# Gate and up projections in seven block products of half width, weight sums formed by adding DMA

## The chip, the cores and the metric

One NeuronCore of a Trainium2 chip runs the whole kernel. The metric is device microseconds of one execution: before the change the median of three runs is 753.54 us (752.19 to 753.91). TensorE is called PE, its weight loads PEld, VectorE DVE, ScalarE ACT, GpSimd POOL and SyncE SP.

## The reference

An encoder block on 512 tokens of width 1024, all in float32: a normed input is projected, goes through two attentions and a gated output projection, and a SwiGLU mixer follows with 2816 inner columns:

```python
h = rms_norm(x, norm_ffn[l])
x = x + (jax.nn.silu(h @ w_gate_ffn[l]) * (h @ w_up_ffn[l])) @ w_down_ffn[l]
```

The change concerns these two lines. The result is the final norm of `x`.

## The kernel before, in words

**Split products.** Every float32 operand is held as two float32r tiles: `hi`, a rounded copy that ACT casts (line 68), and `lo`, the rest, which DVE subtracts (line 75). A product takes three matmuls, hi·hi, hi·lo and lo·hi (`mm3`, lines 88 to 90). `load_unit` (line 77) loads 128x1024 floats of a weight on SP's queue into one of three `raw` buffers and splits it into one of five `whi`/`wlo` pairs of the pool `wp`.

**Before the mixer.** Projections and the attentions come first (group A, then four heads `attend_b`, lines 390 to 421). In a head of `attend_b`, POOL scales the exponentials (line 395), DVE combines two of them (line 399), PE transposes the result (line 361). `weave` (line 439) takes one step of each of several generators in turn, so that the columns of the gates (`gate_col`, line 426, 24 matmuls of 512 columns each) lie between the steps of the heads. The two last heads are woven at lines 465 and 466. Then the output projections follow (lines 488 to 512, 561 to 580); `norm_tile` (line 531) norms one block of 128 tokens, transposes it on PE and leaves its split in `hh` and `hl` (128x8x512: eight blocks of the model width, 512 tokens).

**Gate and up.** `ffn_in` (line 605) makes one of 22 column blocks f of gate and up: for each of the two, eight `mm3` with 512 tokens moving, 48 matmuls in all. For f = 0 and 1 it runs on 256 tokens at a time, so that it can start before the last norm. ACT makes the sigmoid, DVE two products, and the activation block is kept in `acts`.

```python
for f in range(2, NF):
    ffn_in(f, 0, S, *gu(f))
    if f % 2 == 1:
        sums_a(f // 2)
        down0(f // 2 - 1)
```

**Down, in seven products.** The down projection is already done as seven products of 2x2 blocks instead of eight. `sums_a` (line 626) keeps sums of activation blocks in SBUF for each pair of f. `down0` (line 667) loads both column halves of a weight unit, does two of the seven products at once (12 matmuls of 512 columns for each pair of f) and calls `sums_w` (line 647): four DVE differences of 128x512 per pair, each stored from POOL's queue to DRAM (`td`). After the loop `product` (line 704) does the other five products: `weights` loads the sums back, `stat` splits the sums of activations.

**Order.** The program gives each engine its instructions in an order fixed ahead of the run: a planner goes through them in program order as priority, with its own estimates of their times. On the chip every engine works in that order and waits at each instruction for what it needs.

## Time and profile before

| | before |
|---|---|
| median of the runs shown | 753.54 us |
| the profiled execution: its own time | 752.75 us |
| the profiled execution: span of its trace | 751.0 us |
| mean granted PE clock | 0.996 of full speed |
| busy share of the span: PE, PEld | 97%, 83% |
| busy share: DVE, ACT, POOL | 65%, 49%, 17% |
| HBM read, written | 81.20 MB, 13.63 MB |

The span runs from the first to the last instruction. Around it lie 1.75 us (752.75 less 751.0) that the profile does not show, and the profiled execution is 0.79 us below the median. Matmuls are pipelined: the duration of one (389 ns with 512 columns) is longer than the distance between the starts of two, and the distance is what counts for a long row of them.

### The profile page before, as it was taken

The page shows a single profiled execution, that of the slowest core. Times are in us where ns is not written, and L with a number is a line of the kernel's source. Part 1 is how long each engine was busy: PE and PEld are TensorE (multiplying, and loading weights), DVE is VectorE, ACT ScalarE, POOL GpSimd, SP SyncE. Part 2 cuts the span into 40 slices and gives each one's busy share as a digit, 9 for nine tenths or more (in the row PEclk, how much of TensorE's full clock was granted, in tenths as well). Part 3 has the DMA queues.
Part 4 walks back from the last instruction along what each step waited for, and adds up shares of the span by engine and source line. Part 5 has one row for each costly group of instructions (what it writes and reads, how often), then busy time and mean ns, then how long its engine had stood idle before and what let it go on. Part 6 is the DMA issues. An engine that isn't in the chain of part 4 may idle for free.

```text
span 751.0 us, 10105 instructions
## 1 busy us (share of the span) xinstructions
PE 730.7 (97%) x3687; PEld 625.1 (83%) x3687; DVE 491.5 (65%) x811; ACT 367.6 (49%) x664; POOL 128.9 (17%) x170
## 2 busy tenths in 40 slices
...
GB/s 324 79 72 70 57 44 84 1 43 49 65 140 58 57 59 82 168 113 124 143 29 113 224 179 154 145 196 195 168 130 179 196 180 147 215 140 197 190 222 57
DMA packets 29634, 95.50 MB, mean 127 GB/s; under 512 B 3856, under 2 KB 4112, under 8 KB 29584
## 3 DMA queue, kind: packets, MB, share of 16 engines
...
q14 instruction: 21, 0.17, 0.1%
HBM read 81.20 MB, written 13.63 MB: 126 GB/s over the span
## 4 chain that ended last, share of the span: by engine, by line
PE 94%; DVE 2%; DMA 2%; ACT 1%; issue 1%; POOLq 0%; POOL 0%; ACTq 0%; DVEq 0%
PE pu L90 5%; PE pg L90 5%; PE pg L89 5%; PE pu L89 5%; PE pg L88 5%; PE pu L88 5%; PE gt L89 4%; PE gt L88 4%; PE gt L90 4%; PE p L89 3%; PE p L88 3%; PE p L90 3%; PE acc_b L89 3%; PE acc_b L88 3%; PE acc_b L90 3%; PE pp L88 2%
## 5 line engine op out<-in xcount | busy, mean ns | idle before, releaser
L88 PE MATMUL pg<-hh,whi_fg 128*128 128x512 f32 (+1 forms) x192 | 71.4, 372 | 0.0
L90 PE MATMUL pu<-hh,wlo_fu 128*128 128x512 f32 (+1 forms) x192 | 71.4, 372 | 0.0
L89 PE MATMUL pg<-hl,whi_fg 128*128 128x512 f32 (+1 forms) x192 | 71.3, 371 | 0.0
L90 PE MATMUL pg<-hh,wlo_fg 128*128 128x512 f32 (+1 forms) x192 | 71.3, 371 | 0.0
L88 PE MATMUL pu<-hh,whi_fu 128*128 128x512 f32 (+1 forms) x192 | 71.3, 371 | 0.0
L89 PE MATMUL pu<-hl,whi_fu 128*128 128x512 f32 (+1 forms) x192 | 71.3, 371 | 0.0
L654 POOL DMA_DIRECT2D td<-tw x44 | 24.0, 546 | 269.8 <-DVE tw L653 220.4
L68 ACT CAST whi_fg<-raw_fg 128x1024 fp32r<-128x1024 f32 x22 | 23.2, 1054 | 76.9 <-issue 43.4
L68 ACT CAST whi_fu<-raw_fu 128x1024 fp32r<-128x1024 f32 x22 | 23.2, 1054 | 74.1 <-issue 70.1
L88 PE MATMUL gt<-xgh,whi_g 128*128 128x512 f32 x128 | 50.6, 395 | 0.0
L90 PE MATMUL gt<-xgh,wlo_g 128*128 128x512 f32 x128 | 50.5, 395 | 0.0
L89 PE MATMUL gt<-xgl,whi_g 128*128 128x512 f32 x128 | 50.4, 394 | 0.0
L89 PE MATMUL acc_b<-wlo_b,xgh 128*128 128x384 f32 x128 | 43.6, 341 | 0.0
L90 PE MATMUL acc_b<-whi_b,xgl 128*128 128x384 f32 x128 | 43.4, 339 | 0.0
L88 PE MATMUL acc_b<-whi_b,xgh 128*128 128x384 f32 x128 | 43.3, 339 | 0.0
L75 DVE TENSOR_TENSOR wlo_fg<-raw_fg,whi_fg 128x1024 fp32r<-128x1024 f32 x22 | 26.9, 1222 | 24.5 <-ACT whi_fg L68 24.3
L89 PEld LDWEIGHTS pu<-hl,whi_fu 128*128 128x128 f32 x192 | 36.2, 188 | 6.3
L89 PEld LDWEIGHTS pg<-hl,whi_fg 128*128 128x128 f32 x192 | 36.2, 188 | 6.3
L88 PEld LDWEIGHTS pg<-hh,whi_fg 128*128 128x128 f32 x192 | 36.2, 188 | 6.2
L88 PEld LDWEIGHTS pu<-hh,whi_fu 128*128 128x128 f32 x192 | 36.2, 188 | 6.2
L90 PEld LDWEIGHTS pg<-hh,wlo_fg 128*128 128x128 f32 x192 | 36.2, 188 | 6.2
L90 PEld LDWEIGHTS pu<-hh,wlo_fu 128*128 128x128 f32 x192 | 36.2, 188 | 6.2
...
## 6 DMA issues: line engine op xcount, KB each, us to landing
td<-tw POOLq DMA_DIRECT2D x44, 256.0 KB, 4.5
raw_fg<-in_w_gu_dram SPq DMA_DIRECT2D x22, 512.0 KB, 4.4
raw_fu<-in_w_gu_dram SPq DMA_DIRECT2D x22, 512.0 KB, 3.2
raw_t<-td SPq DMA_DIRECT2D x20, 512.0 KB, 3.9
raw_g<-in_w_in_dram SPq DMA_DIRECT2D x16, 512.0 KB, 3.2
...
raw_r<-in_w_down_dram SPq DMA_DIRECT2D x11, 512.0 KB, 4.1
raw_l<-in_w_down_dram SPq DMA_DIRECT2D x11, 512.0 KB, 3.3
```

Of the source, the lines that this page charges most:

```text
L68: a.copy(dst, src)
L75: v.tensor_tensor(out=dst, in0=src, in1=hi.bitcast(F32), op=ALU.subtract)
L88: pe.matmul(acc, lhsT=lh, rhs=rh, start=start, stop=False, skip_group_check=loose)
L89: pe.matmul(acc, lhsT=lh, rhs=rl, start=False, stop=False, skip_group_check=loose)
L90: pe.matmul(acc, lhsT=ll, rhs=rh, start=False, stop=stop, skip_group_check=loose)
L654: g.dma_start(tdram[i][p][:, k * S:(k + 1) * S], t)
```

## The change

The gate and up blocks of f = 2 to 21 are computed as seven products of 2x2 blocks: rows are gate and up, the inner index is halved, and the tokens are halved to 256 (`H`). A product is four `mm3`, 12 matmuls with 256 tokens moving; `g12`, `g5`, `g63`, `g7`, `g4` issue them for one f and the next in turn. Three PSUM banks take part: `q` (two buffers) collects four of the products one after the other and is read out between them. f = 0 and 1 are as before.

The sums of the moving side, `th`/`tl`, are made once after the last norm, at lowered priority (`LATER`). The sums of weights come for each f from two host-made arrays: `w_x0` is loaded on SP's queue, `w_x1` is added to it in SBUF by a DMA on POOL's queue; DVE adds two more, so that three units and a half unit are split per f instead of two.

The sums of the down weights leave DVE: 24 copies from DRAM to DRAM and 24 adding DMAs, all on POOL's queue, in 26 steps, 18 of them woven into the last two heads and 8 before the output projections. The sums of activations are written to DRAM on SP's queue (five stores of 128 KB per pair of f) and loaded again by `stat`. The last product now goes on in the banks `p1` instead of banks of its own. The cut diff:

```diff
...
+    def wblock(i, j, p):
+        n = min(2, NU - 2 * p)
+        return w_down[NU * j + 2 * p:NU * j + 2 * p + n, :, i * S:(i + 1) * S].rearrange("k p s -> p k s")
+
+    def tcopy(i, p, src):
+        return lambda: tc.keep_in_program_order(g.dma_start(tdram[i][p][:, :src.shape[1], :], src))
+
+    def tadd(i, p, src):
+        return lambda: tc.keep_in_program_order(g.dma_start(tdram[i][p][:, :src.shape[1], :], src, accum_op=ALU.add, max_dma_last_dim=4 * S))
+
+    def tsum(i, p):
+        n = min(2, NU - 2 * p)
+        first = (wblock(0, 0, p), wblock(1, 1, p), wblock(0, 1, p), wblock(1, 0, p))[i]
+        second = (wblock(0, 1, p), tdram[0][p][:, :n, :], wblock(1, 1, p), tdram[1][p][:, :n, :])[i]
+        return tcopy(i, p, first), tadd(i, p, second)
+
+    tsums = [tsum(i, p) for i in (0, 2, 1, 3) for p in range(NP)]
+    tsums = [(lambda k=k: [tsums_[k][0]() if k < len(tsums_) else None, tsums_[k - 2][1]() if k > 1 else None]) for tsums_ in [tsums] for k in range(len(tsums) + 2)]
...
-    weave(attend_b(2, *nxt), steps(todo[4:9]))
-    weave(attend_b(3, *nxt1), steps(todo[9:13]))
+    weave(attend_b(2, *nxt), steps(todo[4:9]), steps(tsums[:9]))
+    weave(attend_b(3, *nxt1), steps(todo[9:13]), steps(tsums[9:18]))
...
+        for f in tsums[18 + 2 * qd:20 + 2 * qd]:
+            f()
...
+            a.copy(hraw[2 * (tt // 2) + i][:, :, tt % 2 * P:(tt % 2 + 1) * P], p3)
...
+    with tc.high_priority(offset=-LATER):
+        traw = {"1": hraw[2], "2": hraw[3], "3": hraw[0], "4": hraw[1]}
+        v.tensor_tensor(out=hraw[2], in0=hraw[0], in1=hraw[2], op=ALU.subtract)
+        v.tensor_tensor(out=hraw[3], in0=hraw[3], in1=hraw[2], op=ALU.add)
+        v.tensor_tensor(out=hraw[0], in0=hraw[3], in1=hraw[0], op=ALU.subtract)
+        v.tensor_tensor(out=hraw[1], in0=hraw[3], in1=hraw[1], op=ALU.subtract)
+        for n in "1234":
+            h, l = th[n]
+            if n == "2":
+                split_scaled(h, l, traw[n], -1.0)
+            else:
+                split_hi(h, traw[n])
+                split_lo(l, traw[n], h)
...
+    def load_sums(f):
+        raw = wp.tile([P, UNIT], F32, tag="raw", bufs=3, name=f"raw_a{f}")
+        nc.sync.dma_start(raw, w_gu[2 * f])
+        early = f == 2
+        x = wp.tile([P, UNIT], F32, tag="raw", bufs=3, name=f"x{f}") if early else tp_.tile([P, UNIT], F32, tag="x", bufs=3, name=f"x{f}")
+        nc.sync.dma_start(x, w_x0[f])
+        g.dma_start(x, w_x1[f], accum_op=ALU.add)
+        r22 = tp_.tile([P, S], F32, tag="r22", bufs=3, name=f"r22_{f}")
+        nc.sync.dma_start(r22, w_gu[2 * f + 1][:, S:])
+        hi, lo = split_unit(raw, f"a{f}")
+        w = wts[f] = {"11": (hi[:, :S], lo[:, :S]), "12": (hi[:, S:], lo[:, S:])}
+        hi, lo = split_unit(x, f"x{f}")
+        w["s1"], w["s3"] = (hi[:, :S], lo[:, :S]), (hi[:, S:], lo[:, S:])
+        y = wp.tile([P, UNIT], F32, tag="raw", bufs=3, name=f"y{f}") if early else tp_.tile([P, UNIT], F32, tag="y", bufs=1, name=f"y{f}")
+        v.tensor_tensor(out=y[:, :S], in0=x[:, :S], in1=raw[:, :S], op=ALU.add)
+        v.tensor_tensor(out=y[:, S:], in0=y[:, :S], in1=raw[:, S:], op=ALU.add)
+        hi, lo = split_unit(y, f"y{f}")
+        w["s2"], w["s4"] = (hi[:, :S], lo[:, :S]), (hi[:, S:], lo[:, S:])
+        h = sp_.tile([P, S], F32R, tag="h22", bufs=3, name=f"h22_{f}")
+        l = sp_.tile([P, S], F32R, tag="l22", bufs=3, name=f"l22_{f}")
+        split_hi(h, r22)
+        split_lo(l, r22, h)
+        w["22"] = (h, l)
...
+    hblk = {"11": (hh_[:, 0:4, 0:H], hl_[:, 0:4, 0:H]), "21": (hh_[:, 4:8, 0:H], hl_[:, 4:8, 0:H]), "22": (hh_[:, 4:8, H:], hl_[:, 4:8, H:])}
+    hblk.update({"t" + n: th[n] for n in "1234"})
+
+    def gprod(acc, f, wn, hn, start, stop=False):
+        (wh, wl), (bh, bl) = wts[f][wn], hblk[hn]
+        for k in range(4):
+            c = slice(k * P, (k + 1) * P)
+            mm3(acc, wh[:, c], wl[:, c], bh[:, k, :], bl[:, k, :], start and k == 0, stop and k == 3, True)
+
+    def g12(f):
+        qb[f] = bank("q", f"q{f}", 2)[:, :H]
+        p2 = bank("p2", f"p2_{f}")[:, :H]
+        gprod(qb[f], f, "11", "11", True)
+        gprod(p2, f, "12", "21", True, True)
+        tg[f] = ft.tile([P, S], F32, tag="tg", name=f"tg{f}")
+        a.copy(tg[f][:, :H], qb[f])
+        v.tensor_tensor(out=tg[f][:, :H], in0=p2, in1=tg[f][:, :H], op=ALU.add)
+
+    def g5(f):
+        rb[f] = bank("r", f"r{f}")[:, :H]
+        gprod(rb[f], f, "s1", "t1", True)
+        p5c[f] = ft.tile([P, H], F32, tag="p5", name=f"p5_{f}")
+        a.copy(p5c[f], rb[f])
+
+    def g63(f):
+        gprod(qb[f], f, "s2", "t2", False)
+        a.copy(tg[f][:, H:], qb[f])
+        gprod(rb[f], f, "s4", "22", False, True)
+        v.tensor_tensor(out=tg[f][:, H:], in0=rb[f], in1=tg[f][:, H:], op=ALU.add)
+        sg[f] = ft.tile([P, S], F32, tag="sg", name=f"sg{f}")
+        a.activation(sg[f], tg[f], AF.Sigmoid)
+        v.tensor_tensor(out=sg[f], in0=tg[f], in1=sg[f], op=ALU.mult)
+
+    def g7(f):
+        gprod(qb[f], f, "s3", "t3", False)
+        v.tensor_tensor(out=act_tile(f)[:, H:], in0=qb[f], in1=p5c[f], op=ALU.add)
+        v.scalar_tensor_tensor(out=acts[f][:, H:], in0=acts[f][:, H:], scalar=-1.0, in1=sg[f][:, H:], op0=ALU.mult, op1=ALU.mult)
+
+    def g4(f):
+        gprod(qb[f], f, "22", "t4", False, True)
+        v.scalar_tensor_tensor(out=acts[f][:, :H], in0=qb[f], scalar=-1.0, in1=sg[f][:, :H], op0=ALU.mult, op1=ALU.mult)
+        act_parts(f)
+    def sums_a(u):
+        e, o = acts[2 * u], acts[2 * u + 1]
         p, k = divmod(u, 2)
...
+        s = [sp_.tile([P, M], F32, tag=f"s{i}", name=f"s{i}_{u}") for i in range(4)]
+        v.tensor_tensor(out=s[0], in0=o[:, M:], in1=e[:, M:], op=ALU.subtract)
+        v.scalar_tensor_tensor(out=s[1], in0=s[0], scalar=-1.0, in1=e[:, :M], op0=ALU.mult, op1=ALU.subtract)
+        v.tensor_tensor(out=s[2], in0=e[:, :M], in1=e[:, M:], op=ALU.subtract)
+        v.scalar_tensor_tensor(out=s[3], in0=o[:, :M], scalar=-1.0, in1=s[1], op0=ALU.mult, op1=ALU.subtract)
+        for i, t in enumerate(s + [o[:, M:]]):
+            nc.sync.dma_start(sdram[i][p][:, k, :], t)
...
-        left = load_raw(w_down[u], f"l{u}")
-        hi, lo = split_unit(left, f"d{u}")
-        right = load_raw(w_down[NU + u], f"r{u}", True)
-        sums_w(u, left, right)
+        hi, lo = load_unit(w_down[u], f"d{u}")
...
+    def stat(i, p):
+        n = min(2, NU - 2 * p)
+        raw = tp_.tile([P, S], F32, tag="r22", bufs=3, name=f"sr{i}_{p}")[:, :n * M]
+        nc.sync.dma_start(raw.rearrange("p (k t) -> p k t", t=M), sdram[i][p][:, :n, :])
+        h = sp_.tile([P, S], F32R, tag="h22", bufs=3, name=f"sh{i}_{p}")[:, :n * M]
+        l = sp_.tile([P, S], F32R, tag="l22", bufs=3, name=f"sl{i}_{p}")[:, :n * M]
+        split_hi(h, raw)
+        split_lo(l, raw, h)
         return h, l
...
+    load_sums(2)
+    g12(2)
+    g5(2)
     for f in range(2, NF):
-        ffn_in(f, 0, S, *gu(f))
-        if f % 2 == 1:
+        if f + 1 < NF:
+            load_sums(f + 1)
+        g63(f)
+        if f + 1 < NF:
+            g12(f + 1)
+        else:
+            down0(NU - 2)
+            pr_ = [bank("r", "pr_0"), bank("p2", "pr_1")]
+        g7(f)
+        if f + 1 < NF:
+            g5(f + 1)
+        else:
+            product(0, 0, pr_, True, range(1))
+        g4(f)
+        if f % 2:
             sums_a(f // 2)
-            down0(f // 2 - 1)
-
-    def grab(tag, nm):
-        return [ps_g.tile([P, S], F32, tag=tag, name=f"{nm}_{b}") for b in range(2)]
-
-    pr_ = grab("pg", "pr")
-    product("1", 0, pr_, True, True, range(1))
+            if f + 1 < NF:
+                down0(f // 2 - 1)
...
-    H = S // 2
-    p4 = grab("pu", "p4")
-    half = ps_d.tile([P, S], F32, tag="pd", name="p4_h")[:, :H]
-    outs = [[(p4[0], 0, S)], [(p4[1][:, :H], 0, H), (half, H, S)]]
+    for b in range(2):
+        add(2 + b, S, DM, p1[b], ALU.subtract)
+        finish(2 + b, S, DM, 0)
     NLAST = 2
+    outs = [[(0, S)], [(0, H), (H, S)]]
     for p in range(NP - NLAST):
-        wt, st = weights(3, p), stat("22", p)
+        wt, st = weights(3, p), stat(4, p)
         for b in range(2):
-            for acc, c0, c1 in outs[b]:
-                times(acc, st, wt, p, b, True, False, c0, c1)
+            for c0, c1 in outs[b]:
+                times(p1[b][:, c0:c1], st, wt, p, b, False, True, c0, c1)
+    last = [(weights(3, p), stat(4, p)) for p in range(NP - NLAST, NP)]
     for b in range(2):
-        add(2 + b, 0, S, p1[b])
-        add(2 + b, S, DM, p1[b])
-        finish(2 + b, S, DM, 0)
-    last = [(weights(3, p), stat("22", p)) for p in range(NP - NLAST, NP)]
-    for b in range(2):
-        for i, (acc, c0, c1) in enumerate(outs[b]):
+        for i, (c0, c1) in enumerate(outs[b]):
...
+        "w_x0": np.concatenate([np.concatenate([gu[2 * i + 1][:, :, :512], gu[2 * i][:, :, :512]], axis=2) for i in range(NF)]),
+        "w_x1": np.concatenate([np.concatenate([gu[2 * i + 1][:, :, 512:], gu[2 * i + 1][:, :, :512]], axis=2) for i in range(NF)]),
...
```

## Rows read from the trace of the kernel before

**Rows 1.** Page: busy time (us, share, instructions), and the chain by engine.

```profile
PE 730.7 (97%) x3687; PEld 625.1 (83%) x3687; DVE 491.5 (65%) x811; ACT 367.6 (49%) x664; POOL 128.9 (17%) x170
...
PE 94%; DVE 2%; DMA 2%; ACT 1%; issue 1%; POOLq 0%; POOL 0%; ACTq 0%; DVEq 0%
```

**Rows 2.** Stages: length, busy PE, PEld, DVE, ACT, POOL, clock, DMA share, GB/s.

```profile
235.00:306.00 71.00, 71.00 (x356) 59.25 (x354) 40.52 (x70) 44.25 (x68) 6.02 (x8) 1.00 0.20 67
...
396.20:419.40 23.20, 23.20 (x196) 23.16 (x195) 14.54 (x23) 9.04 (x16) 0.88 (x2) 1.00 0.37 122
419.40:672.00 252.60, 252.60 (x1123) 209.50 (x1122) 141.92 (x206) 77.42 (x109) 22.92 (x43) 1.00 0.52 176
672.00:751.00 79.00, 71.98 (x349) 60.67 (x347) 58.38 (x89) 43.75 (x73) 3.85 (x4) 0.99 0.49 167
```

**Rows 3.** PE timeline, 512 columns (start, duration): first gate, first up matmul.

```profile
431.89 0.39 PE L88 MATMUL pg<-hh,whi_fg 128*128 128x512 f32 x1
...
437.33 0.39 PE L88 MATMUL pu<-hh,whi_fu 128*128 128x512 f32 x1
```

**Rows 4.** PE timeline, 256 columns, f = 1: first gate, first up matmul.

```profile
409.46 0.28 PE L88 MATMUL pg<-hh,whi_fg 128*128 128x256 f32 x1
...
412.35 0.28 PE L88 MATMUL pu<-hh,whi_fu 128*128 128x256 f32 x1
```

**Rows 5.** DVE groups, 419.4 to 672 us (busy, mean ns | idle before).

```profile
L75 DVE TENSOR_TENSOR wlo_fu<-raw_fu,whi_fu 128x1024 fp32r<-128x1024 f32 x19 | 23.1, 1218 | 0.0
...
L618 DVE TENSOR_TENSOR sg<-pu,sg 128x512 f32<-128x512 f32 x20 | 13.8, 688 | 29.9 <-PE pu L90 29.9
...
L75 DVE TENSOR_TENSOR el<-sg,eh 128x256 fp32r<-128x256 f32 x20 | 8.4, 418 | 0.0
...
L653 DVE TENSOR_TENSOR tw<-raw_r,raw_l 128x512 f32<-128x512 f32 x10 | 6.9, 693 | 28.3 <-DMA raw_l<-in_w_down_dram 28.3
L653 DVE TENSOR_TENSOR tw<-raw_r 128x512 f32<-128x512 f32 x10 | 6.9, 692 | 21.7 <-DMA raw_r<-in_w_down_dram 21.7
```

**Rows 6.** DVE timeline: back-to-back operations of 1024 and of 256 columns.

```profile
394.48 1.22 DVE L75 TENSOR_TENSOR wlo_fu<-raw_fu,whi_fu 128x1024 fp32r<-128x1024 f32 x1
395.62 1.22 DVE L75 TENSOR_TENSOR wlo_fg<-raw_fg,whi_fg 128x1024 fp32r<-128x1024 f32 x1
...
409.45 0.75 DVE L618 TENSOR_TENSOR sg<-pu,sg 128x256 f32<-128x256 f32 x2
```

**Rows 7.** DVE timeline: two back-to-back operations of 512 columns.

```profile
440.12 0.68 DVE L653 TENSOR_TENSOR tw<-tw,raw_l 128x512 f32<-128x512 f32 x1
440.73 0.68 DVE L617 TENSOR_TENSOR sg<-pg,sg 128x512 f32<-128x512 f32 x1
```

**Rows 8.** Timeline of all engines, the end: last matmul, reader of its bank.

```profile
743.70 0.28 PE L90 MATMUL p_h<-whi_t,sl 128*128 128x256 f32 x1
...
744.01 0.42 DVE L740 TENSOR_TENSOR x<-x,p_h 128x256 f32<-128x256 f32 x1
```

**Rows 9.** Timeline, attention head: POOL's scaling, DVE behind it, the waiting transpose.

```profile
283.08 0.70 POOL L395 TENSOR_SCALAR p_b_3x<-p_b_3x,r_b_3x 128x512 f32<-128x512 f32 x1 [4.97 <-DVE r_b_3x L355]
...
283.88 0.75 DVE L399 SCALAR_TENSOR_TENSOR p_b_3x<-p_b_3y,c_b,p_b_3x 128x512 f32<-128x512 f32 x1
...
285.10 0.14 PEld L361 LDWEIGHTS ptp_b<-ident,p_b_3x 128*128 128x128 f32 x1
```

**Rows 10.** DVE timeline: the last token block's norm is split.

```profile
407.58 1.29 DVE L75 TENSOR_TENSOR hl<-xt,hh 128x512 fp32r<-128x512 f32 x2 [3.99 <-ACT hh L68]
```

**Rows 11.** Page, part 6: DMA issues (count, KB each, us to landing).

```profile
td<-tw POOLq DMA_DIRECT2D x44, 256.0 KB, 4.5
raw_fg<-in_w_gu_dram SPq DMA_DIRECT2D x22, 512.0 KB, 4.4
```

More of the change, by code (lines that the diff above doesn't have):

```diff
@@ L31 @@
 RIGHT_PAD = 248
+LATER = 400
 @with_exitstack
@@ L43 @@
     w_gu: bass.AP,
+    w_x0: bass.AP,
+    w_x1: bass.AP,
     w_down: bass.AP,
@@ L435, in gate_col @@
         v.tensor_tensor(out=gate[br, qd][:, j, :], in0=acc, in1=rstdB, op=ALU.mult)
+    NU = NF // 2
+    NP = (NU + 1) // 2
+    M = S // 2
+    dr = pool(ctx, "dr", space=bass.MemoryType.DRAM)
+    tdram = [[dr.tile([P, 2, S], F32, name=f"td{i}_{p}") for p in range(NP)] for i in range(4)]
+    def wblock(i, j, p):
[12 more added lines that the diff above has]
+    tsums = [(lambda k=k: [tsums_[k][0]() if k < len(tsums_) else None, tsums_[k - 2][1]() if k > 1 else None]) for tsums_ in [tsums] for k in range(len(tsums) + 2)]
     oA, oB = [], []
@@ L526 @@
     hl_ = hp.tile([P, KT, S], F32R, name="hl")
+    th = {n: (hp.tile([P, 4, S // 2], F32R, name=f"th{n}"), hp.tile([P, 4, S // 2], F32R, name=f"tl{n}")) for n in "1234"}
     np_ = pool(ow, "np", bufs=2, side="right")
-    gffn = np_.tile([P, DM], F32, bufs=1, name="gffn")
+    hraw = [u_tile(f"hraw{i}", F32, (P, 4, S // 2)) for i in range(4)]
+    gffn = u_tile("gffn", F32, (P, DM))
     nc.scalar.dma_start(gffn, norm_ffn.partition_broadcast(P))
@@ L581 @@
     ow.close()
     mixer.close()
-    NU = NF // 2
-    NP = (NU + 1) // 2
-    M = S // 2
+    H = S // 2
     ffn = ExitStack()
-    ap_ = pool(ffn, "ap")
-    sums = {n: ap_.tile([P, NU, M], F32, name=f"s{n}") for n in ("1", "2", "3", "4", "22")}
-    sp_ = pool(ffn, "sp", bufs=3)
-    tp_ = pool(ffn, "tp", bufs=3)
-    dr = pool(ffn, "dr", space=bass.MemoryType.DRAM)
-    tdram = [[dr.tile([P, 2 * S], F32, name=f"td{i}_{p}") for p in range(NP)] for i in range(4)]
+    sp_ = pool(ffn, "sp", bufs=2)
@@ L598 @@
+    tp_ = pool(ffn, "tp", bufs=2)
+    sdram = [[dr.tile([P, 2, M], F32, name=f"sd{i}_{p}") for p in range(NP)] for i in range(5)]
     fin = ExitStack()
     ft = pool(fin, "ft", bufs=2)
+    ep = pool(fin, "ep", bufs=4)
+    actp = pool(fin, "actp", bufs=4)
     ps_d = pool(fin, "ps_d", bufs=4, space=PSUM)
-    ps_g = pool(fin, "ps_g", bufs=2, space=PSUM)
-    raws, acts, parts_a = {}, {}, {}
+    ps_g = pool(fin, "ps_g", space=PSUM)
+    acts, parts_a, wts, qb, rb, tg, sg, p5c = {}, {}, {}, {}, {}, {}, {}, {}
@@ L605, in ffn_in, with bank, act_parts, act_tile @@
+    def bank(tag, nm, bufs=1):
+        return ps_g.tile([P, S], F32, tag=tag, bufs=bufs, name=nm)
+    def act_parts(f):
+        h = ep.tile([P, M], F32R, tag="eh", name=f"eh{f}")
+        l = ep.tile([P, M], F32R, tag="el", name=f"el{f}")
+        split_hi(h, acts[f][:, :M])
+        split_lo(l, acts[f][:, :M], h)
+        parts_a[f] = (h, l)
+    def act_tile(f):
+        acts[f] = actp.tile([P, S], F32, tag="act", name=f"act{f}")
+        return acts[f]
     def ffn_in(f, t0, t1, ug, uu):
@@ L606, in ffn_in @@
         n = t1 - t0
-        pg = ps_g.tile([P, S], F32, tag="pg", name=f"pg{f}_{t0}")[:, :n]
-        pu = ps_g.tile([P, S], F32, tag="pu", name=f"pu{f}_{t0}")[:, :n]
+        pg = bank("q", f"pg{f}_{t0}", 2)[:, :n]
+        pu = bank("p2" if f else "r", f"pu{f}_{t0}")[:, :n]
         for acc, (hi, lo) in ((pg, ug), (pu, uu)):
```

83 lines of the change are left out of this document (22 added, 61 removed).

## The prediction

> **What bounds the kernel now.** I read the page's busy times and its chain first: PE is busy 97% of the span and 94% of the chain is PE's [rows 1]. The busy times by stage say where that holds without a gap: from 235 us to 672 us PE has no idle time at any of the stages shown, while DVE is busy for 141.92 of 252.60 us in the long gate-and-up stage [rows 2]. So a matmul taken out of that stage is worth its whole distance, and any new wait of PE costs its whole length.
>
> What a matmul costs is read from the distance of starts. With 512 columns, 24 matmuls lie between the first gate and the first up matmul of an f: 437.33 less 431.89 is 5.44 us, 226.7 ns each [rows 3]. With 256 columns 24 take 412.35 less 409.46, 2.89 us, 120.4 ns each [rows 4]. Twice 120.4 is 240.8: half-width matmuls lose 6% of what fewer columns win.
>
> **The change part by part.** All terms are set against the profiled execution, 752.75 us (span 751.0 and 1.75 around it), which is 0.79 below the median of 753.54.
>
> *Fewer columns.* Per f, 48 matmuls of 226.7 ns, 10.88 us, become 7x12 = 84 of 120.4 ns, 10.11 us. That is 0.77 us per f and **-15.4 us** for 20 f. The rest of PE's matmuls is unchanged.
>
> The Trainium skill (TensorE: Matmul & The Clock Gate, Back-to-back issue gap) lists 262 cycles for 256 columns and 518 for 512, that is 109.2 and 215.8 ns at 2.4 GHz. By it the same term would be 20 x (10.36 - 9.17) = -23.7 us, an estimate; the rows show 11 ns more per matmul at either length, and the sum goes by the rows.
>
> *DVE's load.* It grows from 6.3 to 9.1 us per f. Operations with nothing to wait for start 1.14 us apart with 1024 columns, 0.33 with 256 [rows 6] and 0.61 with 512 [rows 7]. New per f: 3.5 splits of 1024 (three units and half a down unit), four operations of 512 (split of the half unit, two weight sums, the sigmoid product) and eight of 256 (six around the products, two sums): 3.99 + 2.44 + 2.64 = 9.07. Before, it was 2.5, four and three: 6.28. PE's time per f becomes 10.11 plus 6 down matmuls of 226.7 ns, 11.47 us, so DVE is at 79% and no bound by its mean. ACT stays further below: it was busy 77.42 of 252.60 us [rows 2]. The removed weight differences and their stores lay beside PE and give nothing back.
>
> The Trainium skill (VectorE: DVE Perf Modes, The DRAIN you can't avoid) says that the next operation does not start until the pipe of the one before has emptied. By that DVE would need full durations, 3.5 x 1.218 + 4 x 0.688 + 8 x 0.418 = 10.4 of 11.47 us, an estimate from [rows 5]. The trace disagrees: 1.22 us long operations start 1.13 us apart [rows 6]. Even so DVE would stay under PE's time.
>
> *A new wait of PE on DVE.* `g7` leaves a product in bank `q`, DVE reads it, and only then may `g4` add to the same bank. In between PE has `g5`. From the last `g7` matmul to the first of `g4` lie 13 distances, 1.57 us. DVE starts 0.31 us after the start of a last matmul and takes 0.42 [rows 8]; PE follows a DVE result at most 0.47 us later (283.88 + 0.75 to 285.10 [rows 9]), at least at once. The slack is 0.4 to 0.8, say 0.6 us. A split of 1.14 us that has just begun makes PE late by 0.5; with splits for a third of DVE's time and the slack at times only 0.4, I estimate 0.1 us per f in the mean, so **+2.0 us** with bounds 0 and 11 (0.54 each time). The other readings of these banks have two blocks of 12 matmuls or more (2.9 us) as cover.
>
> *Loads.* Per f, three loads and an adding DMA take the place of two loads. A 512 KB load lands in 4.4 us and a 256 KB store from POOL's queue in 4.5 [rows 11]. The trace shows no adding DMA: it lies between 4.4 and 17.6 (four times, for two reads, a write and both ends in one DMA), and I take 9, twice the 256 KB row of the same queue, since it has twice the bytes. Buffers for three `x` tiles let the load begin more than two f ahead, 23 us, so it costs nothing; without that cover, 4.6 + 9 us once. The five stores per pair on SP wait for DVE, and the next loads are queued behind them; that is covered by the same distance.
>
> *The start.* Four sums of 1024 columns and four splits come after the last norm, whose split starts at 407.58 [rows 10]: 8 x 1.14 = 9.1 us of DVE. In that stage DVE had 14.54 of 23.20 us [rows 2], 8.7 free; `g12(2)` gives 2.9 more, but the sums for f = 2 (a half split more, two weight sums, 1.8) use most of it, and the tiles of the sums lie where `x` for f = 3 goes, so its load starts late. I take **+2.5 us**, bounds 0 and 9.1. The eight copies to `hraw` on ACT lie beside matmuls of the output projection.
>
> *Last product in `p1`.* PE must now wait until DVE has added `p1` to the residual: 0.31, 0.69 [rows 5] and up to 0.47, less the other bank's last three matmuls (0.68): **+0.6 us**, bounds 0 and 1.5.
>
> *Adding DMAs in the heads.* POOL issues 48 DMAs in order. An adding one waits for its copy, issued two steps before; behind it in POOL's queue stand the scalings of the heads, and DVE's combination and the transposes wait for these: 283.08, 283.88, 285.10, with hardly a gap [rows 9]. POOL itself has room: 6.02 of 71 us busy with eight operations [rows 2]. Eighteen steps in 71 us or more are 3.9 us each, so the copy has 7.9 us; with 9 us to land POOL is late by 1.1 us, on eight operations 8.8 at most, most of it beside gate matmuls. I take **+1.5 us**, bounds 0 and 9. A gain is excluded here and at the start: there is only more work.
>
> *Sum.* -15.4 + 2.0 + 2.5 + 0.6 + 1.5 = -8.8; 752.75 - 8.8 = 743.95, and with 0.79 for the median **744.7 us**. This case's own range is 740 to 750: the three waits (DVE, start, heads) together between 2 and 11 us instead of 6.0.
>
> **The rivals.** *All covered.* The planner finds a place for everything: 753.54 - 15.4 + 0.6 = 738.7. For it: DVE's 79%, and a stage that had no idle PE. Against it: a bank that is handed over every 11.47 us with 0.6 us of slack.
>
> *DVE's order binds (slower).* Place: the reading of bank `q` between `g7` and `g4`. DVE works in a fixed order, and in the trace it stands still in it: 29.9 us for `pu`, 28.3 and 21.7 us for two loads, 20 times 2.5 us for the last two [rows 5], harmless since nothing behind them was urgent. With one split and one 512-wide operation ahead of the reading, PE is late by 1.14 + 0.61 - 0.6 = 1.15 us per f, 23 us: 753.54 - 15.4 + 4.6 (the other terms) + 23 = 765.7. It decides from (15.4 - 4.6)/20 = 0.54 us per f on. Against it: the planner sees the dependency and can place the splits.
>
> *Adding DMAs hold up the heads.* If one takes 17.6 us instead of 9, a wait on POOL is 9.7 us; with one such wait uncovered the time is 753.54 - 15.4 + 5.1 + 9.7 = 752.9, no change, and two make it slower. For it: 11.5 MB are copied and as many added (four sums, 11 blocks of 256 KB) while the weights of gates and projections load; 0.52 of the engines at 176 GB/s [rows 2] is 338 GB/s in full, so copies alone are 34 us of all engines. Against it: DMA's share is 0.20 there.
>
> **How the numbers follow.** Forecast 0.47, all covered 0.17, DVE's order 0.22, adding DMAs 0.14. A measurement of this kernel can tell 0.2%, 1.5 us, from no change. Faster: 0.44 of the forecast's, 0.17, and 0.05 of the last, 0.66. Same: 0.03 and 0.04, 0.07. Slower: 0.22 and 0.05, 0.27. The range goes from 738 (all covered, with 0.03 below) to 760, which leaves out the upper half of the DVE case, 0.11, and 0.03 of the last: 0.17 in all.
>
> **What would show it.** Right: 84 matmuls per f at 120 ns; first matmuls of `g4` with gaps of some tenths of a microsecond, released by DVE; a gap of 1 to 4 us between 420 and 435 us; no PE idle in the heads beyond 2 us; a steady period of two f near 23.1 us (2 x 11.47 + 0.2) against 24.48 (96 + 12 matmuls of 226.7 ns). Wrong: a period over 24.48, with PE idle before `g4` or before splits of `x` and `y`; PE idle of over 5 us before 335 us with POOL waiting for DMA; matmuls of 256 columns further apart than 120 ns.

## The result and the profile after

The changed kernel takes **761.04 us** (median of 4 runs, 759.40 to 762.28), the kernel before 753.25 beside it: a ratio of 1.0103 [1.008, 1.0127]. It is slower by 1.0%; 744.7 was forecast, and 761.04 lies just above the range. The profiled execution took 762.28, with a span of 760.5; it is the slowest of the four, so the stages below add up to 9.5 us where the medians differ by 7.8.

The page of the changed kernel (span, busy times, chain by engine), to set against [rows 1]:

```profile
span 760.5 us, 11988 instructions
PE 725.6 (95%) x4407; PEld 652.1 (86%) x4407; DVE 553.2 (73%) x933; ACT 424.7 (56%) x765; POOL 161.7 (21%) x194
...
PE 73%; DMA 13%; DVE 7%; issue 3%; ACT 2%; POOL 1%; ACTq 0%; POOLq 0%; SPq 0%; DVEq 0%
```

PE's share of the chain went from 94% to 73%, and DMA and DVE took most of what it lost: PE now waits for things. The stages, in the columns of [rows 2]:

```profile
235.00:306.00 71.00, 69.94 (x348) 58.17 (x347) 39.11 (x70) 40.69 (x66) 33.02 (x38) 1.00 0.95 234
396.20:419.40 23.20, 21.77 (x159) 20.41 (x159) 15.48 (x21) 12.97 (x23) 1.99 (x3) 1.00 0.36 91
419.40:672.00 252.60, 249.49 (x1917) 242.49 (x1916) 207.60 (x336) 134.70 (x208) 16.21 (x19) 0.99 0.73 208
672.00:760.50 88.50, 74.61 (x347) 61.28 (x345) 58.22 (x90) 44.37 (x73) 4.03 (x4) 0.96 0.66 223
```

Every stage that had PE busy without a gap has one now; DMA's share in the last heads went from 0.20 to 0.95, POOL's busy time from 6.02 to 33.02 us. To place the loss I cut each trace at four PE starts: the first matmul of `oa` (heads), of `pp` (projections, output projection and norm), of `pg` (FFN), and the first on `whi_t` into `p` (the second product of the tail). All lengths in us, the kernels being those of the next section:

| kernel | to `oa` | heads | proj., norm | FFN | tail |
|---|---|---|---|---|---|
| before | 91.51 | 214.80 | 89.92 | 287.26 | 67.51 |
| after | 92.19 | 218.79 | 92.28 | 279.88 | 77.36 |
| e1_no_sum_dma | 91.67 | 214.85 | 89.92 | 281.01 | 74.85 |
| h2_copies | 91.67 | 218.07 | 92.44 | 280.06 | 76.76 |
| h4_thin | 90.48 | 217.45 | 91.91 | 278.71 | 76.45 |
| h1_lag | 92.08 | 217.16 | 101.05 | 280.08 | 77.83 |
| e3_four_full | 91.96 | 218.54 | 92.21 | 273.08 | 76.21 |
| e2_own_banks | 91.78 | 219.22 | 91.93 | 278.96 | 72.81 |
| e4_deep_tail | 91.79 | 218.90 | 92.30 | 279.61 | 72.00 |
| c1_tail | 92.84 | 217.45 | 91.85 | 278.81 | 69.05 |
| c2_tail_four | 91.62 | 218.20 | 92.28 | 273.09 | 68.91 |
| v_none | 91.22 | 214.80 | 89.92 | 273.09 | 68.27 |
| v_late | 91.54 | 214.80 | 110.36 | 273.10 | 68.20 |
| v_ffn | 91.08 | 214.81 | 89.92 | 295.19 | 67.50 |
| v_14 | 90.85 | 214.83 | 89.92 | 273.09 | 67.71 |

Each row is one execution. Where PE has the same instructions in a stage, in the same order, rows still differ: by up to 1.8 us in the heads (217.45 to 219.22), 2.3 us in the FFN (278.71 to 281.01) and 3.0 us in the tail (74.85 to 77.83). So a stage's price is read beside the medians of the runs.

After against before: +0.7 ahead of the heads, **+4.0** in the heads, **+2.4** in projections and norm, **-7.4** in the FFN, **+9.9** in the tail; +9.5 in all, the difference of the spans. From 470 to 662 us PE has no gap; two f take 22.90 us there (starts of the same matmul of `q` at 490.48, 513.38, 536.28) against 24.48. So the saving exists, 0.79 us per f or 15.8 for 20, and 25 us are lost around it. Three places, PE's own timeline (start, duration, in brackets the idle time and what ended it): the end of the heads, the start of f = 3, and the handing over of `p1`.

```profile
304.64 0.39 PE L93 MATMUL gt<-xgh,wlo_g 128*128 128x512 f32 x1
...
307.41 0.49 PE L91 MATMUL ob<-ph_b,vb 128*128 128x512 f32 x1 [0.56 <-ACT ph_b L71]
308.14 0.50 PE L92 MATMUL ob<-pl_b,vb 128*128 128x512 f32 x1 [0.23 <-DVE pl_b L78]
...
310.05 1.05 PE L418 MATMUL pn<-ones,sqb 128*128 128x1 f32 x8 [1.18 <-ACT sqb L415]
...
443.32 0.28 PE L93 MATMUL q<-th,l 128*128 128x256 f32 x1
445.35 0.39 PE L91 MATMUL r<-th,whi_x 128*128 128x256 f32 x1 [1.75 <-ACT whi_x L71]
445.57 0.28 PE L92 MATMUL r<-tl,whi_x 128*128 128x256 f32 x1
446.80 0.58 PE L93 MATMUL r<-th,wlo_x 128*128 128x256 f32 x1 [0.95 <-DVE wlo_x L78]
...
730.33 0.39 PE L93 MATMUL p<-whi_t,sl 128*128 128x512 f32 x1
735.35 0.47 PE L91 MATMUL p<-whi_t,sh 128*128 128x512 f32 x1 [4.64 <-DVE x L848]
```

What DVE did before 735.35, its timeline with the same columns:

```profile
729.92 0.68 DVE L78 TENSOR_TENSOR sl<-sr,sh 128x512 fp32r<-128x512 f32 x1
732.78 1.23 DVE L78 TENSOR_TENSOR wlo_t<-raw_t,whi_t 128x1024 fp32r<-128x1024 f32 x1 [2.17 <-ACT whi_t L71]
733.92 0.69 DVE L78 TENSOR_TENSOR sl<-sr,sh 128x512 fp32r<-128x512 f32 x1
734.52 1.28 DVE L848 TENSOR_TENSOR x<-x,p 128x512 f32<-128x512 f32 x2
```

PE's last matmul into the bank began at 730.33. The add (L848) that empties it stands in DVE's order behind a split that waits for a late weight load, and starts 4.2 us later. PE pays a second time after such gaps, in the clock (length, PE busy, granted clock, DMA share, GB/s). The last two rows are e2_own_banks, which has the same instructions there:

```profile
304.00:308.00 4.00, 3.35 (x16) 1.00 1.07 304
308.00:312.00 4.00, 2.40 (x12) 1.00 1.08 321
312.00:316.00 4.00, 3.76 (x10) 0.58 1.06 362
...
447.00:451.00 4.00, 4.00 (x18) 0.50 1.05 275
451.00:455.00 4.00, 4.00 (x30) 0.80 1.04 407
...
730.00:735.00 5.00, 0.71 (x4) 1.00 1.04 399
735.00:739.00 4.00, 3.65 (x10) 0.61 0.91 355
...
447.00:451.00 4.00, 2.58 (x20) 1.00 1.05 280
451.00:455.00 4.00, 4.00 (x36) 1.00 1.01 386
```

1.00 is the 2.4 GHz level and 0.50 the 1.2 GHz level; a value between them is a window that holds both. After the gaps of the heads 4 us lose 0.42 of their clock (1.7 us); from 443 to 455 us 3.4 us are lost, with 0.85 in 443 to 447 as well; after the gap at 730, 1.7 with the 0.96 that follows. As a reckoning the stages close with that: 5.2 us of gaps (by distances of starts, as all sums of gaps here) and 3.4 of clock in the FFN are 8.6 (15.8 less 7.4 is 8.4), 7.9 of gaps and 1.7 of clock in the tail 9.6 (9.9).

But the clock's 3.4 us in the FFN are not what it costs there. In e2_own_banks PE stops as often (1.12, 0.95, 0.97 and 0.44 us between 443 and 450 us), the clock stays at 1.00, and the FFN is only 0.9 us shorter; in h4_thin and c1_tail, with the clock at 1.00 too, 1.2 and 1.1 us shorter. PE then waits longer for the splits of `y` and `raw_a`: in e2 `q<-th,whi_y` at 448.74 stands 0.97 us for ACT's `whi_y`. So about 1 us of the 8.4 is the clock, and the rest are the waits.

### The profile page after: what moved, and what is told of

It reads as the page before. It is cut to its first block, busy times and chain, and to the rows that moved or that the text cites. A ratio compares the mean times of both kernels' runs of the same rounds, so it can differ in the third digit from the quotient of the medians.

```text
span 760.5 us, 11988 instructions
## 1 busy us (share of the span) xinstructions
PE 725.6 (95%) x4407; PEld 652.1 (86%) x4407; DVE 553.2 (73%) x933; ACT 424.7 (56%) x765; POOL 161.7 (21%) x194
## 4 chain that ended last, share of the span: by engine, by line
PE 73%; DMA 13%; DVE 7%; issue 3%; ACT 2%; POOL 1%; ACTq 0%; POOLq 0%; SPq 0%; DVEq 0%
PE q L91 5%; PE q L92 5%; PE q L93 5%; DMA raw_t<-td 3%; DMA td<-in_w_down_dram 3%; DMA x<-in_w_x_dram 3%; PE acc_b L92 3%; PE acc_b L91 3%; PE acc_b L93 3%; PE gt L91 3%; PE gt L92 3%; PE gt L93 2%; PE r L93 2%; PE p L91 2%; PE r L92 2%
## 5 line engine op out<-in xcount | busy, mean ns | idle before, releaser
L380 POOL TENSOR_SCALAR p_a<-p_a,r_a 128x512 f32<-128x512 f32 x32 | 22.7, 712 | 53.0 <-DVE r_a L358 48.0
L91 PE MATMUL p<-whi_t,sh 128*128 128x512 f32 (+1 forms) x77 | 28.5, 370 | 5.4 <-DVE x L848 5.4
L78 DVE TENSOR_TENSOR wlo_t<-raw_t,whi_t 128x1024 fp32r<-128x1024 f32 (+1 forms) x24 | 27.1, 1131 | 8.5 <-ACT whi_t L71 7.9
L78 DVE TENSOR_TENSOR wlo_y<-y,whi_y 128x1024 fp32r<-128x1024 f32 x20 | 24.4, 1221 | 10.3 <-ACT whi_y L71 10.3
L91 PEld LDWEIGHTS gt<-xgh,whi_g 128*128 128x128 f32 x128 | 24.0, 188 | 6.3 <-DVE gate L438 1.5
L93 PEld LDWEIGHTS gt<-xgh,wlo_g 128*128 128x128 f32 x128 | 24.0, 188 | 5.0
L71 ACT CAST whi_t<-raw_t 128x1024 fp32r<-128x1024 f32 (+1 forms) x24 | 23.2, 976 | 9.0 <-DMA raw_t<-td 8.5
L92 PEld LDWEIGHTS gt<-xgl,whi_g 128*128 128x128 f32 x128 | 24.0, 188 | 4.8
L92 PE MATMUL p<-wlo_t,sh 128*128 128x512 f32 (+1 forms) x77 | 28.1, 366 | 0.0
L452 POOL DMA_DIRECT2D td<-in_w_down_dram x24 | 27.5, 1162 | 0.0
```

Source lines behind the costliest of these rows:

```text
L71: a.copy(dst, src)
L78: v.tensor_tensor(out=dst, in0=src, in1=hi.bitcast(F32), op=ALU.subtract)
L91: pe.matmul(acc, lhsT=lh, rhs=rh, start=start, stop=False, skip_group_check=loose)
L92: pe.matmul(acc, lhsT=lh, rhs=rl, start=False, stop=False, skip_group_check=loose)
L93: pe.matmul(acc, lhsT=ll, rhs=rh, start=False, stop=stop, skip_group_check=loose)
L380: g.tensor_scalar(out=p_, in0=p_, scalar1=r_, scalar2=1.0, op0=ALU.mult, op1=ALU.mult)
```

## The experiments

The first theory had a cause for each of the three places: traffic of the sums in the heads, `x` coming late in the FFN, late loads and the shared bank in the tail. The first four kernels undo one each. The diffs show the decisive places only, at times a part of a line.

**e1_no_sum_dma** (the steps in the projections go too, and `weights` loads plain blocks)

```diff
-    weave(attend_b(2, *nxt), steps(todo[4:9]), steps(tsums[:9]))
-    weave(attend_b(3, *nxt1), steps(todo[9:13]), steps(tsums[9:18]))
+    weave(attend_b(2, *nxt), steps(todo[4:9]))
+    weave(attend_b(3, *nxt1), steps(todo[9:13]))
```

> This run leaves out the sums of the down weights: the 24 copies and 24 adding DMAs of the heads and projections go, and the tail loads plain blocks of w_down in their place (as many bytes, the same instructions). Theory: the heads and projections lost 7 us to DMA traffic, since engines at a share of 0.9 land the weight loads two to three times later and POOL stands on its DMA waits with scalings and norms behind them; so the first FFN product starts near 397 us instead of 403.3 (before 396.2), the DMA share of 235 to 306 us falls from 0.95 to near 0.2, the stalls of TensorE up to 312 us go, and the time falls by 5 to 7 us, to 754 to 756. Rival (the third member of the weave reorders the work of heads, and the traffic itself is harmless): members of the weave are gone as well, so the time falls by as much, but then the late landings are no part of it; a later run with the generator kept and the traffic less decides between them. Second rival (the 7 us come from the new tile layout, hraw copies and th splits): under 1.5 us fall, first FFN product still after 402 us.

754.23 us, ratio to before 0.9996 [0.9979, 1.0012]. First `pg` at 396.44; heads and projections are those of before. Whether traffic or order, this run can't say.

**e2_own_banks**

```diff
+    p4 = [bank("q", f"p4_{b}", 2) for b in range(2)]
+    half = ps_d.tile([P, S], F32, tag="pd", name="p4_h")[:, :H]
-                times(p1[b][:, c0:c1], st, wt, p, b, False, True, c0, c1)
+                times(acc, st, wt, p, b, True, True, c0, c1)
```

> The last product is summed in banks of its own, as in the kernel before, and the hand-over of p1 no longer stands on TensorE's path. Theory: the 4.79 us stall at 730.3 goes and the granted clock of the last 25 us, 0.87, comes back to near 1.00, together 5 to 7 us: 754 to 756. Rival (TensorE's last products are held up by late loads of tdram and sdram anyway, the hand-over only happened to be where the delay was paid): the stall moves to the first matmul on the late weights, and the fall is under 2 us: above 759.

755.60 us, 1.0028 [0.9999, 1.0056]. The tail is 4.6 us shorter. The gap at 730 is gone; in its place are small ones for `sl`, of 0.61 and 0.69 us. One wait of the forecast's kind shows in this run, at the start: the first matmul of `g4` for f = 2 stands 0.37 us for DVE's reading of `q`.

**e3_four_full**

```diff
-        early = f == 2
+        early = False
+    for f in (2, 3):
+        ffn_in(f, 0, S, load_unit(w_gu[2 * f], f"fg{f}"), load_unit(w_gu[2 * f + 1], f"fu{f}"))
-    for f in range(2, NF):
+    for f in range(4, NF):
```

> f = 2 and 3 are computed in eight block products like f = 0 and 1; the loop with seven begins at f = 4, so that x of f = 4 has some 50 us more to be loaded and added. It gives up two seventh-savings, 2 x 0.79 = 1.6 us. Theory (x arrives late, with VectorE's queue behind it): the stalls at 416 to 447 us go (5.2 us) and so does the granted clock of 0.95 between 435 and 475 (2 us), so the time falls by 4 to 7 less 1.6, 2.5 to 5.5 us: 755.5 to 758.5. Rival (the stalls come from VectorE's th splits and sums at the start of the stage, whatever the loads do): they stay, and the time rises by 1.6 us or stays: 761 to 763.

753.84 us, 1.0006 [0.9989, 1.0024]: more than forecast. The FFN stage is 273.08 us without a gap, and that is the ideal: 287.26 less 18 x 0.79 is 273.04. In the changed kernel the load of `x` for f = 3 was issued at 430 us only, since its memory was that of `hraw` until the sums were split, and landed with its add at 444.2; DVE stood for it, with the splits behind it:

```profile
444.25 0.69 DVE L695 TENSOR_TENSOR y<-x,raw_a 128x512 f32<-128x512 f32 x1 [2.53 <-DMA x<-in_w_x_dram]
```

This run needs the first `x` later and gives DVE's start-up splits more cover in one; which of the two counts more it doesn't tell.

**e4_deep_tail**

```diff
-        raw = wp.tile([P, UNIT], F32, tag="raw", bufs=3, name=f"raw_t{i}_{p}")
+        nth[0] += 1
+        raw = (wp if nth[0] % 2 else tp_).tile([P, UNIT], F32, tag="raw" if nth[0] % 2 else "x", bufs=3, name=f"raw_t{i}_{p}")
```

> The tail's weight loads alternate between the three raw buffers and three of x that are free by then, so up to six are under way. Theory (loads of the tail are issued late, because they wait for a buffer, and land late, so VectorE's splits stand before the hand-over's add): raw_t is issued some 15 us earlier, the wait of VectorE before the hand-over goes and the stall of 4.79 us shrinks to under 2; with the clock 4 to 7 us: 754 to 757. Rival (DMA bandwidth: 245 GB/s are all that the traffic of the tail gets): issue is earlier, landing takes longer, the splits come as late as now, and the time moves by less than 2 us.

754.98 us, 1.0013 [0.9997, 1.0029]. The gap at the handing over shrinks from 4.79 to 1.69 us (by starts). The load behind the split at 732.78 was issued at 724.76 us in the changed kernel and landed at 731.62; the same load is issued at 713.76 here and lands at 718.61. So the loads were late because they waited for buffers, not for lack of bandwidth.

**c1_tail**: e2 and e4 together.

> Own banks for the last product and six buffers for the tail's weights, both. Each alone took 5 to 6 us. If they are two ways to take the same stall (VectorE's add of the hand-over behind late splits), both together give little more than one: 753 to 755 us, the tail from the second down product 71 to 72 us long. If loads and hand-over cost each for itself, the tail comes to 67 to 69 us (before 67.5): 750 to 752 us.

752.74 us, 0.9996 [0.9985, 1.0007]; tail 69.05. The two take 4.6 and 5.4 us alone and 8.3 together, of 9.9: each pays mostly for itself. By the medians the two take 5.4 and 6.1 us alone and 8.3 together.

**c2_tail_four**: e2, e3 and e4 together.

> The two edits of the tail and f = 2, 3 in eight products, together. If start of the stage and tail are independent, the 7.2 us of the one and the 6 to 9 us of the others add: 745 to 748 us, below before by 0.8 to 1.1 per cent. If the granted clock or the DMA engines couple them (the loop starts later into the same tail, with the weights of the tail as late), some of it is lost: 748 to 752 us.

745.92 us, 0.9913 [0.9892, 0.9933]. They add, as the table's columns show; the heads' 6 us are left.

For the heads, two kernels change the sums in their place.

**h1_lag** (also the slices of steps: 10, 10 and 3 per `qd`)

```diff
-tsums_[k - 2][1]() if k > 1 else None
+tsums_[k - 8][1]() if k > 7 else None
```

> Each adding DMA is issued eight copies behind its own copy instead of two; bytes, DMAs and the generator in the weave stay. Run without the sums: first FFN product at 396.4 us instead of 403.3. If POOL's standing on its DMA waits (53.3 us in 14 waits, with a scaling of a softmax behind it) is what costs, those waits go, TensorE's stalls between 277 and 312 us go with them, and the first FFN product comes near 397 to 398: 754 to 756 us. If it is the traffic (landing times two to three times longer) or the third generator of the weave, the waits go and the product still starts after 402: 760 to 762 us. If POOL's time for the DMAs themselves (1.3 us each, 27 us more POOL in the last heads), in between.

769.14 us, 1.0203 [1.018, 1.0226]: no theory had that. POOL's timeline and what PE then did:

```profile
319.82 1.04 POOL L455 DMA_DIRECT2D td<-in_w_down_dram  x1 [6.75 <-DMA td<-in_w_down_dram]
320.41 1.50 POOL L111 TENSOR_TENSOR rsb<-ms,mhalf 128x4 f32<-128x4 f32 x1
```

```profile
314.42 0.61 PE L91 MATMUL pp<-oh_b,whi_p 128*128 128x512 f32 x2
321.97 0.80 PE L423 MATMUL pb<-ident,rsb 128*128 128x128 f32 x2 [6.93 <-POOL rsb L111]
```

The norm's `rsb` stood in POOL's queue behind adding DMAs that were waiting, and PE stood for 7.1 us. So POOL's queue can cost what the forecast feared. In the changed kernel such a wait came through too, but small. POOL's longest, 9.8 us up to 270.7, held back a scaling, DVE waited for it and then had work up to a product of the gates that PE needed (timelines of POOL, DVE, PE):

```profile
270.74 1.07 POOL L455 DMA_DIRECT2D td<-in_w_down_dram  x1 [9.78 <-DMA td<-in_w_down_dram]
271.37 1.18 POOL L398 TENSOR_SCALAR p_b_1x<-p_b_1x,r_b_1x 128x512 f32<-128x512 f32 x1
```

```profile
272.58 0.75 DVE L402 SCALAR_TENSOR_TENSOR p_b_1x<-p_b_1y,c_b,p_b_1x 128x512 f32<-128x512 f32 x1 [2.42 <-POOL p_b_1x L398]
...
278.31 1.28 DVE L438 TENSOR_TENSOR gate<-gt,rstdB 128x512 f32<-128x512 f32 x2
```

```profile
279.05 0.50 PE L91 MATMUL gt<-xgh,whi_g 128*128 128x512 f32 x1 [1.06 <-DVE gate L438]
```

In c1_tail, whose heads are the same program, POOL's wait was 7.91 us, DVE's 0.52, and PE had no gap there. So this wait costs 0 to 1.1 us from one execution to the next.

**h2_copies**

```diff
-tsums_[k - 2][1]() if k > 1 else None])
+None])
```

> The 24 copies stay and the 24 adding DMAs are left out (this leaves the second term of every down-weight sum out). POOL then waits for no DMA and has half the DMA instructions; about half the traffic stays. Theory (POOL's waits and DMA instructions hold up the scalings): first FFN product at 397 to 398 us, 754 to 756 us. Rival (traffic): about half of the 7 us stays, 399 to 401 and 757 to 759 us. Rival (the third generator reorders the weave): it is still there, so nothing changes: after 402 and 760 to 762 us.

760.60 us, 1.0088 [1.0063, 1.0114]: POOL waits for no DMA any more, DMA's share in 235 to 306 us is 0.53 instead of 0.95, and yet heads and projections lose 5.8 of the 6.4 us. Of the three readings, the one that the sums alter the order is left. In the traces PE's, DVE's and ACT's instructions in the heads stand in one order before and in e1, and in another in the changed kernel and here: the planner, which is free to move work, put the last head's steps later and the gates earlier (why it did, presumably since its own reckoning has POOL taken by the DMAs, was not tried). In the trace above the last gate matmul starts at 304.64 and the last head's transposes, splits and `ob` follow with nothing beside them. In e1 gates lie between all of them, up to the last norm:

```profile
301.17 0.39 PE L92 MATMUL ob<-pl_b,vb 128*128 128x512 f32 x1
301.40 0.39 PE L93 MATMUL ob<-ph_b,vb 128*128 128x512 f32 x1
301.63 0.39 PE L91 MATMUL gt<-xgh,whi_g 128*128 128x512 f32 x1
...
305.48 0.39 PE L93 MATMUL gt<-xgh,wlo_g 128*128 128x512 f32 x1
305.71 0.95 PE L418 MATMUL pn<-ones,sqb 128*128 128x1 f32 x8
```

**h4_thin**: h2 with the copies cut, so that the order stays and the bytes go.

```diff
-g.dma_start(tdram[i][p][:, :src.shape[1], :], src)
+g.dma_start(tdram[i][p][:, :src.shape[1], :8], src[:, :, :8])
```

> The changed kernel with its 24 copies cut to 8 of 512 columns, and without the adding DMAs; the tail loads plain blocks of w_down, so the down-weight sums are left out. The instruction order of TensorE, VectorE and ScalarE in the heads is that of the changed kernel, the bytes of the copies are 1/64. If the order costs (the last head's chain without gate products to cover it): first projection at 309 to 311 us, first FFN product at 401 to 403, 759 to 761 us. If traffic costs: product at 396.4 to 398, 754 to 755 us.

759.48 us, 1.0077 [1.0056, 1.0098]. Its profiled execution, 756.80, is the shortest of six, in part for an early start; by stages heads and projections still lose 2.65 and 2.0, that is 4.6 of 6.4 us, at a DMA share of 0.26. POOL's issuing of 24 small DMAs is still in it (POOL is busy 14.66 us in 235 to 306, against 6.22 in e1), but its gaps, at 304.37, 305.09 and 307.00, are ended by ACT and DVE as in the changed kernel, and POOL starts nothing between 286.06 and 309.30. The six kernels with the full sums in the heads and PE's instructions there in this same order (after, e2, e3, e4, c1, c2) lose between 4.6 and 6.5 us; c1_tail, with all the traffic, loses 4.6 as h4 does. So 4.6 us come with the order. On top come the gap near 279 us, and in h2 a clock at 0.50 from 308.4 to 315.2 us; beyond these no run shows a price of the bytes in the heads.

Then the sums were placed where they leave that order alone. All four have the edits of c2.

**v_none**: without the sums, the floor.

> The last kernel (two edits of the tail, f = 2 and 3 in eight products: 745.92 us, first FFN product at 402.1) without copies and adding DMAs; plain blocks of w_down are loaded in the tail, so the down-weight sums are left out. This is the floor for any other placing of them. If the heads' loss is independent of the other two, the product starts at 396.4 and the run takes 6 to 7 us less: 739 to 740. If the clock or the tail take some of it back: 741 to 744.

739.63 us, 0.9817 [0.9802, 0.9832].

**v_late**

```diff
-    for f in todo[13:]:
+    for f in todo[13:] + tsums[0:6]:
-        for f in tsums[18 + 2 * qd:20 + 2 * qd]:
+        for f in tsums[6 + 5 * qd:11 + 5 * qd]:
```

> The kernel of 745.92 us with all 24 copies and 24 adding DMAs moved behind the heads, into the projections (306 to 396 us). In the instruction order of the compiled program TensorE's work up to the first projection is then that of the kernel before, instruction by instruction, while with the sums in the heads it was another; the copies alone kept that other order and nearly the whole loss. Theory now (what cost in the heads is the other order, which leaves the last head's chain without cover; traffic is cheap): first projection at 306.5 instead of 309.8, TensorE's stalls at 305 to 311 us gone, first FFN product at 397 to 399, 741 to 743 us. Rival (traffic and POOL's waits): the projections now carry it all, DMA share about 1 there, weight loads late; the loss moves there and the product starts at 402 or later: 746 us or more.

759.40 us, 1.0076 [1.0059, 1.0092]: the theory's first half held, its time did not. Heads take 214.80 again, and from 306 to 383 us PE loses nothing beside a DMA share of 1.01: traffic alone is harmless there. Then the norm's `r` stands in POOL's queue behind the adding DMAs, as `rsb` did in h1. The timelines of DVE and PE:

```profile
399.75 1.28 DVE L571 SCALAR_TENSOR_TENSOR xn<-x,r,gffn 128x1024 f32<-128x1024 f32 x1 [19.33 <-POOL r L111]
```

```profile
401.18 1.09 PE L576 MATMUL xt<-ident,xn 128*128 128x128 f32 x4 [17.43 <-DVE xn L571]
```

**v_ffn** (no steps in heads and projections; each add eight copies behind its copy)

```diff
         if f + 1 < NF:
             load_sums(f + 1)
+            for fn in tsums[0 + 2 * (f - 4):2 + 2 * (f - 4)]:
+                fn()
```

> The kernel of 745.92 us with the sums moved into the FFN loop, two copies and two adding DMAs per f from f = 4, each add eight copies behind its copy. The order up to the first FFN product is that of the kernel before. If the loss was order, the product starts at 396.4. In the loop the DMA share goes from 0.73 to about 0.9 with VectorE at 82 per cent; if x still comes in time (it landed 5 to 9 us after its load, an f takes 11.4 us), nothing is lost there: 739 to 741 us, below the kernel before by 1.7 to 1.9 per cent. If the traffic makes x or the raw loads late, the steady state gets stalls of TensorE and part of it is lost: 742 to 750.

762.21 us, 1.0113 [1.0094, 1.0133]. Heads, projections and tail are as good as they get; the FFN stage loses 22 us. Its DMA share is above 1 (columns as in [rows 2]), and the loads land late (queue, count, KB each, us to landing, from 500 to 600 us):

```profile
470.00:660.00 190.00, 174.53 (x1322) 168.37 (x1321) 136.85 (x228) 88.89 (x139) 44.40 (x51) 0.96 1.03 285
...
raw_a<-in_w_gu_dram SPq DMA_DIRECT2D x7, 512.0 KB, 18.3
x<-in_w_x_dram SPq DMA_DIRECT2D x7, 512.0 KB, 19.6
x<-in_w_x_dram POOLq DMA_DIRECT2D x7, 512.0 KB, 13.3
```

In the changed kernel the three take 4.6, 4.7 and 5.5 us there. `x` with its add now takes 33 us, against some 23 that three buffers give. That adds of the sums hold up those of `x` in POOL's queue, the rival of v_14's expectation, doesn't show: none of POOL's waits from 470 to 660 us is for a `td`. In v_14 the same three loads take 7.6, 7.9 and 6.9 us.

**v_14**: between the two limits, 14 steps in the projections, 12 in the loop, none in the heads.

```diff
+    for f in todo[13:] + tsums[0:2]:
+        for f in tsums[2 + 3 * qd:5 + 3 * qd]:
+            if f in [4, 6, 8, 10, 12, 14, 15, 16, 17, 18, 19, 20]:
+                tsums[14 + [4, 6, 8, 10, 12, 14, 15, 16, 17, 18, 19, 20].index(f)]()
```

> The kernel of 745.92 us with 14 of the 26 steps of sums moved into the projections and 12 into the FFN loop, one at f = 4, 6, 8, 10, 12 and at each f from 14 to 20. With all 26 steps in the projections TensorE lost nothing until 383 us, 14 steps were through by 373 us, and POOL's work for the norm begins at 380.7; a step took about 3.6 us of full DMA engines, so one in two f of 11.4 us raises the share in the loop from 0.75 by 0.16. If these two limits are all there is, first FFN product at 396 to 397, no stall of TensorE in the loop, 739 to 742 us, 1.5 to 1.9 per cent below the kernel before. If adds on POOL's queue hold up the adds of x behind them, stalls appear in the loop: 743 to 750 us.

**739.55 us**, ratio to before **0.981 [0.979, 0.983]**, faster than both kernels and level with the floor: the sums cost nothing any more. Its page and two stages, in the columns used above:

```profile
span 736.4 us, 11810 instructions
PE 716.6 (97%) x4335; PEld 644.1 (87%) x4335; DVE 543.6 (74%) x919; ACT 418.9 (57%) x755; POOL 159.7 (22%) x192
...
PE 94%; DMA 2%; DVE 2%; ACT 1%; issue 0%; POOLq 0%; POOL 0%; ACTq 0%; SPq 0%; DVEq 0%
```

```profile
306.00:396.00 90.00, 90.00 (x412) 74.85 (x411) 52.38 (x69) 29.69 (x39) 25.59 (x30) 1.00 0.85 246
419.40:657.00 237.60, 237.60 (x1765) 227.82 (x1764) 190.16 (x308) 121.37 (x187) 34.07 (x40) 1.00 0.92 261
```

The chain is PE's at 94% again, the clock 1.00, with DMA at 0.92 in the loop. All it gains on before, 14.2 us, is 18 x 0.79.

## Why the prediction was wrong

*Fewer columns*, -15.4: right, 15.8 by the period. The pitch read from [rows 3, 4] held in blocks of another make, and v_14 shows the term bare. (The prediction's "lose 6% of what fewer columns win" doesn't follow from its figures: 84 matmuls at half of 226.7 ns would take 9.52 us, so of 1.36 us per f that fewer columns could save, the longer distance takes 0.59. The -15.4 is right all the same.) The gaps that the Trainium skill lists (TensorE: Matmul & The Clock Gate, Back-to-back issue gap) would have given -23.7; the measurement decides for the rows.

*DVE's load*: DVE was busy 82%, near the 79% forecast. The section of the Trainium skill cited there (VectorE: DVE Perf Modes, The DRAIN you can't avoid) itself excepts an operation that isn't held back by the one before it; so the starts 1.14 us apart in [rows 6] (1.13 in the prediction) do not speak against it.

*A new wait of PE on DVE*, +2.0 with bounds 0 and 11: nothing, the lower bound. PE has no gap between `g7` and `g4` from 470 to 662 us, with DVE busy for 207.60 of 252.60 us from 419.4. The rival of DVE's order, 765.7, came nearer the time than the forecast, by luck as to the place: nothing was lost between `g7` and `g4`. Its mechanism, DVE standing in its fixed order, is the one that struck in the tail.

*The start*, +2.5 with bounds 0 and 9.1: it cost 8.4. The two causes, DVE's splits and a late `x` for f = 3, were both named, but priced as DVE's work alone; the wait for `x` (2.53 us of DVE at 444.25) with DVE's queue behind it, and about 1 us of clock, were not. How the 8.4 divide between splits and `x` stays open.

*Last product in `p1`*, +0.6 with bounds 0 and 1.5: the step that failed most. It took DVE as free to read the bank at once. The add stands in DVE's order behind splits that wait for loads, and starts 4.2 us after the last matmul. The prediction had read in [rows 5] that DVE stands still in its order for loads, 28.3 and 21.7 us, and used it for bank `q` alone; a row for `p1` itself was not to be had, since before, the last product had banks of its own. The handing over and the loads behind it make up most of the tail's 9.9 us: own banks take back 4.6, six buffers 5.4, both 8.3 (5.4, 6.1 and 8.3 by the medians). That the tail's loads grew (the statistics come back from DRAM through three buffers) had no term at all.

*Adding DMAs in the heads*, +1.5 with bounds 0 and 9: 6.4, inside the bounds, but for the most part by another way. The forecast's own way, POOL late behind an adding DMA, DVE behind POOL and PE behind DVE, did occur and cost 1.1 us in the profiled execution, near the 1.5, and nothing in c1_tail, though POOL's waits were many (53.3 us in 14). 4.6 of the 6.4 us come with the other order of the heads' instructions. The forecast took the order of the heads as fixed, though its own account of the kernel says that a planner sets it.

*What no term held*: the granted clock behind a gap, 1.7 us in the projections, 1.7 in the tail by the reckoning above, and about 1 in the FFN. A gap was costed at its length. The price stood in the trace of before, ahead of the rows that the forecast looked at, where PE starts again (PE timeline, then length, PE busy, granted clock, DMA share, GB/s):

```profile
21.16 0.50 PE L90 MATMUL akv<-whi_akv,xgl 128*128 128x256 f32 x2 [3.98 <-DVE xgl L72]
```

```profile
21.80:25.20 3.40, 3.40 (x18) 0.50 0.03 7
```

The sign was lost because the forecast counted 6.6 us against the saving and 25 came. The term that it feared most, DVE between `g7` and `g4`, came to nothing, and the tail, of which it had the handing over alone, at 0.6, cost most, 9.9.
